# g_mem inside the memory chunks, row blocks turned between products, identity transposes ahead of the first product

## The chip, the cores and the metric

The kernel runs on one core of a Trainium2 chip. The metric is the device time of one execution in microseconds, median of three runs. The engines have short names in the profile: PE is TensorE (PEld its weight loads), DVE VectorE, ACT ScalarE, POOL GpSimd, SP SyncE, which issues most DMA transfers.

## The reference

One decoder layer in float32: a sequence of 512 rows of 1024 columns (`x`), and 256 memory rows (`mem`). The lines that the change touches:

```python
h = rms_norm(x, g_mix[l])
proj = h @ w_in[l]
q, k, v, qi, ki, wi, conv_in, qc, gate_pre = split_cols(proj, PROJ_SIZES)
qi = partial_rope(qi.reshape(b, s, N_IDX_HEADS, IDX_DIM), cos_i, sin_i)
ki = partial_rope(ki, cos_i, sin_i)
y_att = dsa_attention(q, k, v, qi, ki, wi) @ w_att_out[l]
mem_kv = (rms_norm(mem, g_mem[l]) @ w_mem_kv[l]).reshape(b, m, 2, N_CROSS_HEADS, HEAD_DIM)
y_mem = memory_attention(qc, mem_kv[:, :, 0], mem_kv[:, :, 1]) @ w_mem_out[l]
```

Behind them come a short convolution branch, three gates, the output product `w_o`, and a gated convolutional MLP (`w_up`, `w_down`). `rms_norm(x, g)` is `x * rsqrt(mean(x*x) + eps) * g`.

## The kernel before

Every matrix product is made of three TensorE matmuls (`mm3`, L145): both operands are split into a rounded half `hi` (ScalarE) and a remainder `lo` (VectorE), and hi x hi, hi x lo and lo x hi are added in one PSUM bank. A split (`split`, L155) is so one ScalarE and one VectorE instruction.

The work around the change is the start of the kernel, some 46 us:

- **Memory chunks.** `m_kv` holds, for each of the eight blocks of 128 rows of the contraction, 256 columns of `mem` transposed and 512 columns of `w_mem_kv`. It comes in five transfers (L255): the first two blocks singly, the others in pairs, called the first to fourth chunk here. For each block ScalarE and VectorE multiply the memory half by `gm`, a column of `g_mem` (L280, L281), and split the weights; then six products add to two banks `pkv`, one for each block of 128 memory rows. The norm's factor is put on later, in `memory_out` (L296).
- **Row blocks.** `x` comes in four blocks of 128 rows (`xin`). `norm_rows` (L165) normalises one: a sum of squares on ScalarE (L160), two small GpSimd steps (L161, L162), and one VectorE instruction (L170) that writes `xn`. `turn_rows` (L173) transposes it on TensorE, eight 128x128 transposes into two `at` banks, and splits the result into `h`. Block 0 is normalised and turned amid the memory chunks, block 1 behind them.
- **Row products.** The loop over b at L321 multiplies each block by `w_n`: 24 matmuls of 424 columns into a `mm` bank `pn`, which hold V, the index queries and keys, and the index weights `wiN`. At its end the loop normalises and turns block b + 2. ScalarE rounds V, copies the index rows to `rn` (L335), VectorE rotates them with the table `ropeN` in six small instructions (L338 to L343), and TensorE turns the result: the keys (L346, 32 columns) for each block, the queries (L349) for all but block 0. For blocks 0 and 1, `memory_out` is called as well, and its sum of squares over a memory block is the ScalarE instruction `rows<-rows` at L160.
- Behind it the first products with `w_in` begin (the operands come from `ahead`, L309); from there on TensorE runs the long products.

The order on each engine is set by a scheduler that places instructions by a simulated time and by priority (`tc.high_priority` raises the normalisation and the splits), except where `tc.keep_in_program_order` pins one: a pinned instruction isn't moved across the others of its engine that stand ahead of it in the program. An engine runs its instructions strictly in the order so made. DMA transfers use eight completion semaphores in turn, so that a transfer waits for the one eight places ahead of it.

Of the kernel before, what the change touches and what calls it, by code (L numbers as in the profile page):

```python
# [17 lines left out]
P = 128  # L18
S = 512
NB = S // P  # L20
# [72 lines left out]
@with_exitstack  # L93
def layer(ctx, tc, x, mem, g_mix, g_mem, g_ffn, g_final, w_in, w_n, m_kv, w_cm, w_att, w_o, w_up, w_down,
          params, rope, rope_n, out):
# [48 lines left out]

    def mm3(o, sh, sl, mh, ml, first, last):  # L145
        nc.tensor.matmul(o, sh, mh, start=first, stop=False)  # L146
        nc.tensor.matmul(o, sh, ml, start=False, stop=False)  # L147
        nc.tensor.matmul(o, sl, mh, start=False, stop=last)  # L148
# [23 lines left out]

    def turn_rows(xn, dst, b, tag="at"):  # L173

        for h in range(2):
            pt = bank(tag)
            for k in range(4):
                nc.tensor.transpose(pt[:, k * P:(k + 1) * P], xn[:, (4 * h + k) * P:(4 * h + k + 1) * P], ident)
            pv = pt.rearrange("p (k s) -> p k s", s=P)
            split(dst[0][:, 4 * h:4 * h + 4, b * P:(b + 1) * P], dst[1][:, 4 * h:4 * h + 4, b * P:(b + 1) * P], pv)  # L180
# [46 lines left out]
    ea = es.enter_context(pool("ea", side="right"))  # L227
    gm = ea.tile([P, KD], F32, name="gm")
    gx = ea.tile([P, D], F32, name="gx")
    ropeN = ea.tile([P, 2, NB, 4], F32, name="ropeN")  # L230
    nc.scalar.dma_start(gm, g_mem)
    nc.scalar.dma_start(ropeN, rope_n)

    warm = const.tile([P, 1], F32, name="warm")
    tc.keep_in_program_order(nc.scalar.activation(warm, mhalf, AF.Copy))


    def first(dma):
        tc.keep_in_program_order(dma)
# [10 lines left out]
    for c in range(KD // 2):  # L250

        n = 1 if c == 0 else 2
        raw = op.tile([P, 2, M + 2 * CW], F32, tag=kv_tags[c], name="mkv")
        for i in range(0, 2, n):
# [16 lines left out]
    xin.append(first_rows(x, 3, ea, "in3"))  # L271
    memn.append(first_rows(mem, 1, op, "omel"))


    pkv = [bank("o"), bank()]
    for c, (raw, hi, lo, n) in enumerate(mkv):
        for i in range(0, 2, n):
            for k in range(2 * c + i, 2 * c + i + n):
                src = raw[:, k % 2, :M]
                nc.scalar.activation(mh[:, k], src, AF.Copy, scale=gm[:, k:k + 1])  # L280
                nc.vector.scalar_tensor_tensor(ml[:, k], src, gm[:, k:k + 1], mh[:, k].bitcast(F32), op0=ALU.mult,  # L281
                                               op1=ALU.subtract)
            split(hi[:, i:i + n], lo[:, i:i + n], raw[:, i:i + n, M:])
            for k in range(2 * c + i, 2 * c + i + n):
                for b in range(MB):
                    bs = slice(b * P, (b + 1) * P)
                    mm3(pkv[b], mh[:, k, bs], ml[:, k, bs], hi[:, k % 2], lo[:, k % 2], k == 0, k == KD - 1)
        if c == 2:
            norm_T(xin[0], gx, h, 0, ea)
# [31 lines left out]
    for b in range(NB):  # L321
        bs = slice(b * P, (b + 1) * P)
        pn = bank()
        for i in range(4):
            for j in range(2):
                k = 2 * i + j
                mm3(pn[:, :NW], h[0][:, k, bs], h[1][:, k, bs], wn[i][1][:, j], wn[i][2][:, j], k == 0, k == KD - 1)
        if b + 2 < NB:
            with tc.high_priority(offset=800):
                norm_T(xin[b + 2], gx, h, b + 2, ea)  # L330
        split(V[:, b, :, 0:HD], V[:, b, :, HD:], pn[:, :KV].rearrange("p (g d) -> p g d", g=NG))
# [537 lines left out]
```

## Time and profile before

| | us |
|---|---|
| median of three runs | 756.78 (756.10 to 756.96) |
| profiled execution, its own time | 757.61 |
| span of the profiled execution | 755.8 |
| TensorE busy in the span | 740.9 |
| VectorE, ScalarE, GpSimd busy | 464.5, 340.2, 21.1 |

The profiled execution is 0.83 us above the median, and its span, from the first to the last instruction, is 1.8 us shorter than its own time. In the rows below, times are from the span's start; a matmul's duration includes the fill and drain of the array, so that consecutive matmuls overlap, and the distance of their starts is what one costs.

### The profile page before, as it was taken

The page shows a single profiled execution, that of the slowest core. Times are in us where ns is not written, and L with a number is a line of the kernel's source. Part 1 is how long each engine was busy: PE and PEld are TensorE (multiplying, and loading weights), DVE is VectorE, ACT ScalarE, POOL GpSimd, SP SyncE. Part 2 cuts the span into 40 slices and gives each one's busy share as a digit, 9 for nine tenths or more (in the row PEclk, how much of TensorE's full clock was granted, in tenths as well). Part 3 has the DMA queues.
Part 4 walks back from the last instruction along what each step waited for, and adds up shares of the span by engine and source line. Part 5 has one row for each costly group of instructions (what it writes and reads, how often), then busy time and mean ns, then how long its engine had stood idle before and what let it go on. Part 6 is the DMA issues. An engine that isn't in the chain of part 4 may idle for free.

```text
span 755.8 us, 9168 instructions
## 1 busy us (share of the span) xinstructions
PE 740.9 (98%) x3458; PEld 618.9 (82%) x3458; DVE 464.5 (61%) x795; ACT 340.2 (45%) x568; POOL 21.1 (3%) x49
## 2 busy tenths in 40 slices
PE   6999999999999999999999999999999999999996
PEld 4888888888888888888899888888888888888884
DVE  4845999999777763386466565656565654121225
ACT  5848565676455553244235434343434443121214
POOL 0200002000000000000010000000000000000001
PEclk9999999999999999999999999999999999999998
DMA  9625234522122224344403232232323232323202
GB/s 340 221 84 172 85 111 123 170 72 76 57 91 74 74 65 161 117 139 138 142 29 99 97 97 100 91 104 88 107 86 110 83 112 76 119 84 109 86 29 112
DMA packets 25709, 81.81 MB, mean 108 GB/s; under 512 B 3424, under 2 KB 4576, under 8 KB 25664
## 3 DMA queue, kind: packets, MB, share of 16 engines
q1 hardware_dynamic: 25232, 80.94, 32.7%
q8 instruction: 27, 0.44, 0.3%
q10 hardware_dynamic: 432, 0.28, 0.1%
q14 instruction: 18, 0.15, 0.1%
HBM read 75.77 MB, written 2.10 MB: 103 GB/s over the span
## 4 chain that ended last, share of the span: by engine, by line
PE 94%; ACT 2%; DMA 1%; DVE 1%; POOL 1%; issue 1%; POOLq 0%; SPq 0%
PE ps_mm L146 19%; PE ps_mm L148 19%; PE ps_mm L147 19%; PE ps_at L146 9%; PE ps_at L148 9%; PE ps_at L147 9%; PE ps_at L625 1%; PE ps_o L656 1%; DMA mkv<-m_kv 1%; PE ps_o L147 1%; PE ps_o L148 1%; PE ps_o L146 1%; PE ps_at L642 1%; PE ps_at L420 1%; PE ps_at L556 1%
## 5 line engine op out<-in xcount | busy, mean ns | idle before, releaser
L157 DVE TENSOR_TENSOR wlo<-raw,whi 128x1024 fp32r<-128x1024 f32 (+2 forms) x122 | 144.7, 1188 | 197.1 <-ACT whi L156 197.1
L156 ACT ACTIVATE whi<-raw 128x1024 fp32r<-128x1024 f32 (+2 forms) x122 | 125.8, 1032 | 177.1 <-PE ps_o L148 82.1
L146 PE MATMUL ps_mm<-hhi,whi 128*128 128x512 f32 x312 | 122.8, 394 | 0.0
L147 PE MATMUL ps_mm<-hlo,whi 128*128 128x512 f32 x312 | 122.2, 392 | 0.0
L148 PE MATMUL ps_mm<-hhi,wlo 128*128 128x512 f32 x312 | 122.2, 392 | 0.0
L147 PE MATMUL ps_at<-h2l,whi 128*128 128x512 f32 (+1 forms) x216 | 78.9, 366 | 0.0
L148 PE MATMUL ps_at<-h2h,wlo 128*128 128x512 f32 (+1 forms) x216 | 78.8, 365 | 0.0
L146 PE MATMUL ps_at<-h2h,whi 128*128 128x512 f32 (+1 forms) x216 | 78.7, 366 | 0.0
L148 PEld LDWEIGHTS ps_mm<-hhi,wlo 128*128 128x128 f32 x312 | 58.6, 188 | 11.7
L147 PEld LDWEIGHTS ps_mm<-hlo,whi 128*128 128x128 f32 x312 | 58.6, 188 | 11.6
L146 PEld LDWEIGHTS ps_mm<-hhi,whi 128*128 128x128 f32 x312 | 58.6, 188 | 11.5
L146 PE MATMUL ps_mm<-h2h,whi 128*128 128x512 f32 x160 | 62.2, 389 | 0.0
L147 PE MATMUL ps_mm<-h2l,whi 128*128 128x512 f32 x160 | 62.2, 389 | 0.0
L148 PE MATMUL ps_mm<-h2h,wlo 128*128 128x512 f32 x160 | 62.2, 389 | 0.0
L147 PEld LDWEIGHTS ps_at<-h2l,whi 128*128 128x128 f32 x216 | 40.7, 189 | 6.6
L148 PEld LDWEIGHTS ps_at<-h2h,wlo 128*128 128x128 f32 x216 | 40.7, 189 | 6.5
L146 PEld LDWEIGHTS ps_at<-h2h,whi 128*128 128x128 f32 x216 | 40.6, 189 | 6.5
L147 PEld LDWEIGHTS ps_mm<-h2l,whi 128*128 128x128 f32 x160 | 30.0, 188 | 6.3
L148 PEld LDWEIGHTS ps_mm<-h2h,wlo 128*128 128x128 f32 x160 | 30.0, 188 | 6.2
L146 PEld LDWEIGHTS ps_mm<-h2h,whi 128*128 128x128 f32 x160 | 30.0, 188 | 6.2
L789 ACT ACTIVATE t<-t 128x512 f32<-128x512 f32 x22 | 13.9, 633 | 44.9 <-DVE t L471 44.8
L156 ACT ACTIVATE acth<-t 128x512 fp32r<-128x512 f32 x14 | 8.8, 632 | 40.4 <-DVE t L790 40.4
(266 smaller groups left out, 1316.8 us busy)
## 6 DMA issues: line engine op xcount, KB each, us to landing
raw<-w_up SPq DMA_DIRECT2D x44, 512.0 KB, 3.4
raw<-w_in SPq DMA_DIRECT2D x39, 512.0 KB, 3.4
raw<-w_down SPq DMA_DIRECT2D x22, 512.0 KB, 3.4
raw<-w_o SPq DMA_DIRECT2D x8, 512.0 KB, 3.5
raw<-w_cm SPq DMA_DIRECT2D x8, 320.0 KB, 3.0
mkv<-m_kv SPq DMA_DIRECT2D x3, 768.0 KB, 8.8
rows<-x SPq DMA_DIRECT2D x4, 512.0 KB, 10.1
x<-x SPq DMA_DIRECT2D x4, 512.0 KB, 6.4
```

The lines of the kernel that those rows point to most:

```text
L146: nc.tensor.matmul(o, sh, mh, start=first, stop=False)
L147: nc.tensor.matmul(o, sh, ml, start=False, stop=False)
L148: nc.tensor.matmul(o, sl, mh, start=False, stop=last)
L156: nc.scalar.activation(hi, src, AF.Copy)
L157: nc.vector.tensor_sub(lo, src, hi.bitcast(F32))
L420: nc.tensor.matmul(pb[:, :W], Q4[:, hd, (b - 1) * P:b * P], K4[:, :W], start=True, stop=True)
L556: nc.tensor.matmul(pb[:, j * M:(j + 1) * M], QC[:, 2 * t + j, b * P:(b + 1) * P], KM[i][:, 2 * t + j, :], start=(i == 0), stop=(i == 1))
L625: nc.tensor.matmul(pb[:, :N], QS[:, hd, b * P:(b + 1) * P], KS[i][:, g, :N], start=(i == 0), stop=(i == 1))
L642: nc.tensor.transpose(pt[:, kb * P:(kb + 1) * P], lt[:, kb * P:(kb + 1) * P], ident)
L656: nc.tensor.matmul(po[:, q0:], V[:, kb, g, :], PT[i][:, c], start=(kb == 0 and i == 0), stop=(kb == NB - 1 and i == 1))
L789: nc.scalar.activation(tt[0], tt[0], AF.Silu)
```

## The change

Four edits, all in the start of the kernel:

1. `g_mem` is no longer a table of its own. Each row of `m_kv` gets one more column that holds it, so that a row is 769 instead of 768 numbers long; the instructions at L280 and L281 (L287, L288 after) read the factor from the chunk. The transfer of the table on ScalarE's queue is gone.
2. The transfer of the index rope table `ropeN` moves from the front of ScalarE's queue to the end of the start-up loads on SyncE's, behind the last memory block and ahead of the parameters `par`.
3. Fifteen TensorE transposes of the identity into an `at` bank that nothing reads stand ahead of the first product.
4. Blocks 2 and 3 are normalised in the loop rounds b = 1 and b = 2, ahead of that round's products, and turned in the middle of them, behind the first 12 (before: at the end of rounds 0 and 1). The first transpose of each half, and the first matmul behind the turn, are pinned to their place in the program.

```diff
--- before.py
+++ after.py
@@ -91,7 +91,7 @@
 
 
 @with_exitstack
-def layer(ctx, tc, x, mem, g_mix, g_mem, g_ffn, g_final, w_in, w_n, m_kv, w_cm, w_att, w_o, w_up, w_down,
+def layer(ctx, tc, x, mem, g_mix, g_ffn, g_final, w_in, w_n, m_kv, w_cm, w_att, w_o, w_up, w_down,
           params, rope, rope_n, out):
     nc = tc.nc
 
@@ -142,8 +142,10 @@
     def wrows(w, r, sp=wp):
         return wsplit(w[r * P:(r + 1) * P, :].rearrange("p (k c) -> p k c", c=P), sp)
 
-    def mm3(o, sh, sl, mh, ml, first, last):
-        nc.tensor.matmul(o, sh, mh, start=first, stop=False)
+    def mm3(o, sh, sl, mh, ml, first, last, pin=False):
+        mm = nc.tensor.matmul(o, sh, mh, start=first, stop=False)
+        if pin:
+            tc.keep_in_program_order(mm)
         nc.tensor.matmul(o, sh, ml, start=False, stop=False)
         nc.tensor.matmul(o, sl, mh, start=False, stop=last)
 
@@ -170,12 +172,14 @@
         nc.vector.scalar_tensor_tensor(xn, src, r, g, op0=ALU.mult, op1=ALU.mult)
         return xn
 
-    def turn_rows(xn, dst, b, tag="at"):
+    def turn_rows(xn, dst, b, tag="at", pin=False):
 
         for h in range(2):
             pt = bank(tag)
             for k in range(4):
-                nc.tensor.transpose(pt[:, k * P:(k + 1) * P], xn[:, (4 * h + k) * P:(4 * h + k + 1) * P], ident)
+                mm = nc.tensor.transpose(pt[:, k * P:(k + 1) * P], xn[:, (4 * h + k) * P:(4 * h + k + 1) * P], ident)
+                if pin and k == 0:
+                    tc.keep_in_program_order(mm)
             pv = pt.rearrange("p (k s) -> p k s", s=P)
             split(dst[0][:, 4 * h:4 * h + 4, b * P:(b + 1) * P], dst[1][:, 4 * h:4 * h + 4, b * P:(b + 1) * P], pv)
 
@@ -225,14 +229,16 @@
 
     es = ExitStack()
     ea = es.enter_context(pool("ea", side="right"))
-    gm = ea.tile([P, KD], F32, name="gm")
     gx = ea.tile([P, D], F32, name="gx")
     ropeN = ea.tile([P, 2, NB, 4], F32, name="ropeN")
-    nc.scalar.dma_start(gm, g_mem)
-    nc.scalar.dma_start(ropeN, rope_n)
 
     warm = const.tile([P, 1], F32, name="warm")
     tc.keep_in_program_order(nc.scalar.activation(warm, mhalf, AF.Copy))
+
+
+    idle = bank("at")
+    for i in range(15):
+        nc.tensor.transpose(idle[:, :P], ident, ident)
 
 
     def first(dma):
@@ -250,7 +256,7 @@
     for c in range(KD // 2):
 
         n = 1 if c == 0 else 2
-        raw = op.tile([P, 2, M + 2 * CW], F32, tag=kv_tags[c], name="mkv")
+        raw = op.tile([P, 2, M + 2 * CW + 1], F32, tag=kv_tags[c], name="mkv")
         for i in range(0, 2, n):
             first(nc.sync.dma_start(raw[:, i:i + n], m_kv[2 * c + i:2 * c + i + n].rearrange("k p c -> p k c")))
         hi = wp.tile([P, 2, 2 * CW], F32R, tag="whi", name="whi", bufs=3)
@@ -270,17 +276,18 @@
     memn = [first_rows(mem, 0, op, "omeh")]
     xin.append(first_rows(x, 3, ea, "in3"))
     memn.append(first_rows(mem, 1, op, "omel"))
+    first(nc.sync.dma_start(ropeN, rope_n))
 
 
     pkv = [bank("o"), bank()]
     for c, (raw, hi, lo, n) in enumerate(mkv):
         for i in range(0, 2, n):
             for k in range(2 * c + i, 2 * c + i + n):
-                src = raw[:, k % 2, :M]
-                nc.scalar.activation(mh[:, k], src, AF.Copy, scale=gm[:, k:k + 1])
-                nc.vector.scalar_tensor_tensor(ml[:, k], src, gm[:, k:k + 1], mh[:, k].bitcast(F32), op0=ALU.mult,
+                src, gm = raw[:, k % 2, :M], raw[:, k % 2, M + 2 * CW:]
+                nc.scalar.activation(mh[:, k], src, AF.Copy, scale=gm)
+                nc.vector.scalar_tensor_tensor(ml[:, k], src, gm, mh[:, k].bitcast(F32), op0=ALU.mult,
                                                op1=ALU.subtract)
-            split(hi[:, i:i + n], lo[:, i:i + n], raw[:, i:i + n, M:])
+            split(hi[:, i:i + n], lo[:, i:i + n], raw[:, i:i + n, M:M + 2 * CW])
             for k in range(2 * c + i, 2 * c + i + n):
                 for b in range(MB):
                     bs = slice(b * P, (b + 1) * P)
@@ -321,13 +328,18 @@
     for b in range(NB):
         bs = slice(b * P, (b + 1) * P)
         pn = bank()
+        nxt = xin[b + 1] if 0 < b < NB - 1 else None
+        if nxt is not None:
+            with tc.high_priority(offset=800):
+                nxt = norm_rows(nxt, gx, ea)
         for i in range(4):
+            if nxt is not None and i == 2:
+
+                turn_rows(nxt, h, b + 1, "at", pin=True)
             for j in range(2):
                 k = 2 * i + j
-                mm3(pn[:, :NW], h[0][:, k, bs], h[1][:, k, bs], wn[i][1][:, j], wn[i][2][:, j], k == 0, k == KD - 1)
-        if b + 2 < NB:
-            with tc.high_priority(offset=800):
-                norm_T(xin[b + 2], gx, h, b + 2, ea)
+                mm3(pn[:, :NW], h[0][:, k, bs], h[1][:, k, bs], wn[i][1][:, j], wn[i][2][:, j], k == 0, k == KD - 1,
+                    pin=nxt is not None and k == 4)
         split(V[:, b, :, 0:HD], V[:, b, :, HD:], pn[:, :KV].rearrange("p (g d) -> p g d", g=NG))
         nc.vector.tensor_scalar_mul(wiN[:, b, :], pn[:, NW - NIH:NW], (NIH * IDXD) ** -0.5)
         rn = ea.tile([P, NIH + 1, IDXD], F32, tag="rn", name="rn", bufs=2)
@@ -845,14 +857,14 @@
     add("x", w["x"])
     add("mem", w["mem"])
     add("g_mix", w["g_mix"].reshape(1, D))
-    add("g_mem", w["g_mem"].reshape(KD, P).T)
     for n in ("g_ffn", "g_final"):
         add(n, w[n].reshape(1, D))
     wide = range(0, D, P)
     add("w_in", col_blocks(w["w_in"], IN_STARTS))
     add("w_n", np.stack([col_blocks(w["w_in"][i:i + 2 * P], [C_V], NW)[0] for i in range(0, D, 2 * P)]))
 
-    add("m_kv", np.concatenate([w["mem"].reshape(M, KD, P).transpose(1, 2, 0), w["w_mem_kv"].reshape(KD, P, 2 * CW)], axis=2))
+    add("m_kv", np.concatenate([w["mem"].reshape(M, KD, P).transpose(1, 2, 0), w["w_mem_kv"].reshape(KD, P, 2 * CW),
+                                w["g_mem"].reshape(KD, P, 1)], axis=2))
     add("w_cm", np.concatenate([col_blocks(w["w_conv_out"], wide), col_blocks(w["w_mem_out"], wide)], axis=2))
     add("w_att", col_blocks(w["w_att_out"], range(0, D, 2 * P), 2 * P))
     add("w_o", w["w_o"])
```

TensorE in the loop over row blocks, around the turn of block 2, in the kernel before (`wnh`, `wnl` are the split of `w_n`, `rn` the rotated index rows, here of block 0, `xn` the normalised block):

```order
L147 MATMUL ps_mm<-wnl_155,hhi 128x424
L148 MATMUL ps_mm<-wnh_154,hlo 128x424
L178 MATMUL ps_at<-ident,xn 128x128 x8
L346 MATMUL ps_at<-ident,rn 32x128
L178 MATMUL ps_at<-ident,xn 128x128 x4
L146 MATMUL ps_mm<-wnh_142,hhi 128x424
L147 MATMUL ps_mm<-wnl_143,hhi 128x424
L178 MATMUL ps_at<-ident,xn 128x128 x4
```

The same place after the change:

```order
L149 MATMUL ps_mm<-wnl_160,hhi 128x424
L150 MATMUL ps_mm<-wnh_159,hlo 128x424
L358 MATMUL ps_at<-ident,rn 32x128
L180 MATMUL ps_at<-ident,xn 128x128 x8
L146 MATMUL ps_mm<-wnh_163,hhi 128x424
L149 MATMUL ps_mm<-wnl_164,hhi 128x424
L150 MATMUL ps_mm<-wnh_163,hlo 128x424
```

Before, all of block 1's products (the last with `wnh_154`) stand ahead of the turn of block 2 and of L346, and the turn of block 3 is broken by block 2's first products. After, only 12 of block 1's 24 products stand ahead, then L358 (L346 before), then the turn of block 2, then block 1's other 12 products.

VectorE at the same time, before:

```order
L365 TENSOR_SCALAR par<-par 128x24
L170 SCALAR_TENSOR_TENSOR xn<-rows,st,gx 128x1024
L338 TENSOR_TENSOR rt<-rn,ropeN 128x36
L339 TENSOR_TENSOR rt<-rn,ropeN 128x36
L341 TENSOR_TENSOR rn<-rn,ropeN 128x9x4
L340 TENSOR_TENSOR rn<-rn,ropeN 128x9x4
L343 TENSOR_TENSOR rn<-rn,rt 128x9x4
L342 TENSOR_TENSOR rn<-rn,rt 128x9x4
```

And after:

```order
L377 TENSOR_SCALAR par<-par 128x24
L350 TENSOR_TENSOR rt<-rn,ropeN 128x36
L351 TENSOR_TENSOR rt<-rn,ropeN 128x36
L353 TENSOR_TENSOR rn<-rn,ropeN 128x9x4
L352 TENSOR_TENSOR rn<-rn,ropeN 128x9x4
L172 SCALAR_TENSOR_TENSOR xn<-rows,st,gx 128x1024
L355 TENSOR_TENSOR rn<-rn,rt 128x9x4
L354 TENSOR_TENSOR rn<-rn,rt 128x9x4
```

The normalisation of row block 3 (`xn`) moves from ahead of block 0's rotation to between its fourth and its fifth step. On ScalarE the sums of squares of a memory block and of the row block beside it change places, twice: `rows<-rows` now stands ahead of `xn<-rows`. Behind the first group of `w_in` products all engines have the same order in both kernels.

## Rows read from the trace of the kernel before

**Rows 1.** The page: span, TensorE, its clock by slice, the second small DMA queue.

```profile
span 755.8 us, 9168 instructions
...
PE 740.9 (98%) x3458; PEld 618.9 (82%) x3458; DVE 464.5 (61%) x795; ACT 340.2 (45%) x568; POOL 21.1 (3%) x49
...
PEclk9999999999999999999999999999999999999998
...
q10 hardware_dynamic: 432, 0.28, 0.1%
```

**Rows 2.** Stretches: length; PE, PEld, DVE, ACT, POOL busy (instructions); PEclk, DMA share, GB/s.

```profile
4.80:10.90 6.10, 5.49 (x12) 3.80 (x12) 2.64 (x6) 2.88 (x5) 0.00 (x0) 1.00 1.02 374
...
18.00:20.00 2.00, 1.61 (x9) 1.08 (x8) 1.77 (x2) 2.00 (x5) 0.22 (x2) 1.00 1.03 419
...
45.50:748.50 703.00, 703.00 (x3279) 586.61 (x3277) 434.95 (x733) 310.75 (x511) 13.38 (x27) 1.00 0.31 100
748.50:751.00 2.50, 0.01 (x1) 0.00 (x0) 1.54 (x5) 1.26 (x4) 0.73 (x1) 1.00 0.53 210
751.00:752.00 1.00, 0.00 (x0) 0.00 (x0) 0.75 (x1) 0.72 (x1) 0.20 (x1) 0.71 0.02 8
```

**Rows 3.** Timeline, TensorE, start: start, duration, line, operation, [idle before <- releaser].

```profile
4.83 0.79 PE L146 MATMUL ps_o<-whi,mT 128*128 128x512 f32 x1 [4.83 <-ACT mT L280]
...
9.69 0.63 PE L148 MATMUL ps_mm<-whi,mT 128*128 128x512 f32 x1
10.94 0.50 PE L146 MATMUL ps_o<-whi,mT 128*128 128x512 f32 x1 [0.62 <-ACT whi L156]
...
12.20 0.50 PE L147 MATMUL ps_o<-wlo,mT 128*128 128x512 f32 x1 [0.53 <-DVE wlo L157]
```

**Rows 4.** Timeline, GpSimd's identity and ScalarE's second chunk.

```profile
1.14 0.29 POOL masks.py:199 TENSOR_SCALAR_AFFINE_SELECT ident<-ident 128x128 f32<-128x128 f32 x1
...
9.04 0.91 ACT L280 ACTIVATE mT<-mkv,gm 128x256 fp32r<-128x256 f32 x2 [3.20 <-DMA mkv<-m_kv]
```

**Rows 5.** Timeline, TensorE, the row blocks' products and turns.

```profile
27.77 0.55 PE L148 MATMUL ps_mm<-wnh,hlo 128*128 128x424 f32 x2
...
29.91 0.35 PE L146 MATMUL ps_mm<-wnh,hhi 128*128 128x424 f32 x1
...
32.23 1.04 PE L178 MATMUL ps_at<-ident,xn 128*128 128x128 f32 x8
33.11 0.27 PE L346 MATMUL ps_at<-ident,rn 128*32 128x128 f32 x1
...
34.93 0.46 PE L146 MATMUL ps_mm<-wnh,hhi 128*128 128x424 f32 x1 [1.12 <-ACT hhi L156]
...
45.56 0.39 PE L147 MATMUL ps_mm<-hlo,whi 128*128 128x512 f32 x1
45.79 0.40 PE L148 MATMUL ps_mm<-hhi,wlo 128*128 128x512 f32 x1
```

**Rows 6.** Timeline, ScalarE, GpSimd and VectorE around block 0's index rows.

```profile
30.33 0.20 ACT L160 ACTIVATION_READ_ACCUMULATOR rows<-rows 128x1 f32 x1
30.43 0.41 ACT L335 ACTIVATE rn<-ps_mm 128x288 f32<-128x288 f32 x1
...
29.58 0.19 POOL L161 TENSOR_SCALAR st<-st 128x1 f32<-128x1 f32 x1 [2.17 <-ACT xn L160]
29.86 0.55 POOL L162 TENSOR_TENSOR st<-st,mhalf 128x1 f32<-128x1 f32 x1
30.62 1.16 POOL L161 TENSOR_SCALAR st<-st 128x1 f32<-128x1 f32 x1 [0.21 <-ACT rows L160]
...
30.44 1.28 DVE L170 SCALAR_TENSOR_TENSOR xn<-rows,st,gx 128x1024 f32<-128x1024 f32 x1 [1.21 <-POOL st L162]
31.64 0.19 DVE L338 TENSOR_TENSOR rt<-rn,ropeN 128x36 f32<-128x36 f32 x1
...
32.24 0.19 DVE L342 TENSOR_TENSOR rn<-rn,rt 128x36 f32<-128x36 f32 x1
```

## The prediction

> **What bounds the kernel now.** The page comes first: TensorE is busy for 740.9 of the span's 755.8 us [rows 1]. The table of stretches then says where it isn't: from 45.5 to 748.5 us it is busy for all 703.0 us, so whatever TensorE loses or gains before 45.5 us reaches the end one for one, and nothing later takes it up [rows 2]. The change works only ahead of that point, so I read the first 46 us row by row. There TensorE loses time in three places. It has nothing until 4.83 us. It waits at 10.94 and 12.20 us for the second memory chunk [rows 3], and that wait goes back to a transfer: ScalarE sat 3.20 us until the chunk landed at 9.04 us [rows 4]. Last, at 34.93 us, it waits 1.12 us for the ScalarE half of row block 2's split, right after turning that block [rows 5]. The profiled execution lasted 757.61 us with its span of 755.8; the median of the three runs is 756.78. I make the sum as a difference on the span and put it on the median.
>
> **The identity transposes.** The first 12 products (those of the first two chunk rows) start at 4.83 and the last of them at 9.69 us, 0.44 us apart; later ones are 0.23 us apart (45.56 to 45.79) [rows 3, 5]. The page's clock row and the stretch 4.80 to 10.90 both print full clock there [rows 1, 2], but 512 columns in 0.43 us is the lower level of 1.2 GHz, and 0.23 us is the 2.4 GHz one. So the low clock costs 12 x 0.20 = 2.4 us of TensorE time. None of that is on the path: if the 12 products took 2.7 us instead of 5.1, TensorE would be done near 8 us and still could not go on before 10.94 us, because the chunk lands at 9.04 us and its first multiply-and-round and its split take until 10.9 us [rows 3, 4]. Gain taken: 0. The price of the 15 transposes themselves: the identity is written at 1.43 us [rows 4]; eight transposes at the high clock start 0.11 us apart (32.23 to 33.11) [rows 5], so 15 at half the clock take about 3.3 us and end near 4.9 us, 0 to 0.4 us after the operands; the slack of 0.62 us ahead of 10.94 us hides that [rows 3]. The transposes are TensorE's own; no other engine waits for them.
>
> The Trainium skill's page "TensorE: Matmul & The Clock Gate", in Part 4 on transposes, says that transpose mode does not count as TensorE activity for the clock in the way matmuls do. No row of before shows the clock's answer to transposes alone. By that rule the first 12 products stay slow and the sum of this part is the same 0, since the wait for the chunk takes up either case; what it alters is the chance of the clock rival below, where transposes follow a wait.
>
> **g_mem in the chunks, the rope table last.** Two ScalarE-queue transfers of 128 small packets each go away at the front, 16 KB of them come back at the end of the start-up queue, ahead of the parameters. All small packets of that queue, with the last output among them, are 432 packets in 0.1% of sixteen engines' span [rows 1], so 0.75 us at most for all, of which the two tables can be some 0.2 us; that comes off the landing of every chunk. Against it the chunk's rows grow from 3072 to 3076 bytes. Rows of w_n, 3392 bytes, move at 419 GB/s between 18 and 20 us, no slower than anything else [rows 2]; I take 0, with 0.4 us as the dear end (5% of the four chunks of 768 KB at that rate). The table now follows the load of the last memory block on SyncE's queue; ScalarE takes that block's sum of squares ahead of the copy at 30.43 us, and the table, 16 KB, is first read after that copy (31.64 us before) [rows 6], so it isn't late. Sum taken: -0.1 us, from -0.4 to +0.4.
>
> The page "DMA: Bandwidth & Descriptors", section "How a descriptor splits into AXI transactions", of the Trainium skill says that a descriptor which does not start on a 256-byte boundary spends extra beats. An estimate from it is about 4 beats on 96, near 0.4 us by the fourth chunk, which would be the dear end; the 419 GB/s of the 3392-byte rows speak against it.
>
> **Row blocks turned amid the products.** This part decides. In the order of before, TensorE runs all 24 products of block 1, turns block 2, and only then turns the rotated index row of block 0 (L346). In the new order the first of the pinned transposes keeps its program place, and so everything that stands ahead of it in the program must run ahead of it: the transpose of block 0's rotated keys, L358, now comes after only 12 of block 1's products, and the turn of block 2 and all else queues behind it. TensorE gets there at 29.91 us (the thirteenth product's start in before) [rows 5]. Are the rotated keys ready? Follow the chain. Block 0's last product starts at 27.77 us [rows 5]. After rounding its V, ScalarE's order holds two sums of squares (now memory block 1 first, row block 3 second) ahead of the copy L347, so that the copy runs at 30.43 us as before and the second sum is read out at 30.53 us [rows 6]. VectorE's order now holds four of the six rotation steps, then the normalisation of row block 3, then the last two steps, where before all six stood together. The normalisation waits for GpSimd, whose two steps for the row sum before took 0.83 us (29.58 to 29.86 + 0.55) [rows 6]: 30.6 + 0.85 = 31.45 us. The normalisation takes 1.20 us of VectorE (30.44 to 31.64), the last two steps 0.3 us (32.24 us is the start of the last, and each starts 0.11 us after the other) [rows 6]: 31.5 + 1.2 + 0.3 = 33.0 us. With the hand-over L358 starts at 33.05 us. **The wait is 33.05 - 29.91 = 3.1 us.** Its bounds: 1.75 us if the normalisation cost nothing (copy 30.43 + 0.41, six steps of 0.12, a hand-over), 4.1 us if GpSimd's first step takes the 1.16 us that it took beside a VectorE normalisation [rows 6].
>
> What goes away: from 29.91 to 45.56 us are 15.65 us [rows 5]. The work in it is 60 products of 424 columns, 11.6 us at 0.194 (the starts at 27.77 and 29.91 are 11 products apart) [rows 5], 16 turns at 0.11 = 1.8, four rotated-row turns 0.35, one product of 512 columns 0.23: 14.0 us. So before loses 1.65 us there, 1.12 in the wait at 34.93 and the rest in restarts after waits. After: that goes, since 12 products (2.3 us) now stand between the turn and its first reader, twice the 1.12 us that it waited. In comes 3.1 us, and some 0.3 us for restarts. For block 1's rotated rows, ahead of the turn of block 3, the same chain without sums or normalisation in it is about 2.2 us against 2.3 us of products: 0 to 0.2 us, 0.1 taken. **Sum: +3.1 + 0.3 + 0.1 - 1.65 - 0.1 = +1.75 us, which gives 756.78 + 1.75 = 758.5 us.** Behind L358 nothing but TensorE's own queue waits; ScalarE and VectorE have the first w_in split to do meanwhile.
>
> **Rivals.** (1) The wait is there and the clock falls in it. After the last product of the kernel (about 748.5 us) the clock was lower from within 751 to 752 us on, after less than 3 us without a matmul [rows 2]; a wait of 3.1 us followed by 1 us of transposes is of that size. Against it: waits of 0.62 and 1.12 us left the clock up. Its price: a 424-column product takes 0.35 instead of 0.19 us, and if the low clock lasts as long as at the start, 5.5 us or 15 products, that is 2.4 us; half of it is possible. 760.0 to 761.0 us, 760.4 as its own time. The Trainium skill's page "TensorE: Matmul & The Clock Gate", section "HAM oscillation — how this bites in real kernels", says that where matmul bursts are parted by long enough waits, each next burst starts slow; the end of this trace agrees, with the fall to 1.2 GHz after under 3 us of no matmul.
>
> (2) The change does what it is named for and the rope rows are there in time: the 1.65 us of lost time goes, 0.1 us on the transfers, and nothing new comes. 755.0 us. For it: the 1.12 us wait is real and 12 products would cover it. Against it: the copy L347 cannot run before ScalarE has done the two sums, so that L358 is late by 1.75 us even at the lower bound; it decides only if L358's operand is ready by 31.5 us.
>
> (3) The wait comes out at its lower end, near 2 us, because VectorE finishes the rotation before GpSimd is done, or the start gains up to 0.4 us: 756.5 to 757.8 us, no change that can be told.
>
> (4) The faster first 12 products leave TensorE idle for some 2 to 3 us ahead of 10.94 us, and the clock falls there, so that the products from 12.20 us on start slow: up to 2.4 us on top of the forecast, 1.8 taken. 760.3 us.
>
> **How the numbers follow.** Forecast, the wait with the clock up: 45%, 758.5 us, its own range 757.8 to 759.4. Rival 1: 32%. Rival 4: 5%. Rival 3: 12%. Rival 2: 6%. The range from 757.2 to 761.2 us leaves out rival 2, half of rival 3 and the upper tail of the clock. About 0.2%, 1.5 us, is what a measurement of this kernel can tell from no change; the forecast lies just beyond it, so a third of its 45% counts as no change. Slower 0.67, the same 0.26, faster 0.07.
>
> **What would show it.** In the trace of the changed kernel: the first 12 products 0.43 or 0.23 us apart, and the next one at 10.5 to 11.3 us either way; L358 starting 2 to 4 us after the product ahead of it, released by VectorE's L354 or L355, with VectorE's normalisation L172 between L352 and L355; no wait of over 0.3 us ahead of block 2's first product; the spacing of the 424-column products after L358, 0.19 us (forecast) or 0.35 us (rival 1). The forecast falls if L358 waits less than 1.5 us, or if TensorE isn't busy throughout after 48 us.

## The result, and the profile after

The changed kernel takes 761.66 us (median; 759.87 to 761.73) where the kernel before takes 756.87 beside it: a ratio of 1.0059, with a 95% interval from 1.0042 to 1.0076. That is slower by 3.2 to 5.8 us. The direction was forecast, the size (+1.75 us) wasn't, and the time lies above the range. The profiled execution took 761.6 us with a span of 759.8. Two executions of the experiments below, of 829.8 us (e7) and 4286.69 us (e11), lie far outside the rest and are in no ratio.

The page, as in [rows 1]: the span, and TensorE with its share.

```profile
span 759.8 us, 9193 instructions
...
PE 744.6 (98%) x3473; PEld 622.2 (82%) x3473; DVE 464.9 (61%) x795; ACT 340.6 (45%) x568; POOL 20.1 (3%) x49
```

TensorE is busy 3.7 us longer than before, but 3.46 us of that are the 15 new transposes at the start, in time that was idle before. So the sum of the busy time doesn't price the loss, which must be looked for in the distance of the starts as well as in idle time.

The start, TensorE in order of time (start, duration, line, operation, idle before and what ended it), answering to [rows 3]:

```profile
1.48 3.46 PE L241 MATMUL ps_at<-ident 128*128 128x128 f32 x15 [1.48 <-POOL ident masks.py:199]
4.96 0.80 PE L146 MATMUL ps_o<-whi,mT 128*128 128x512 f32 x1
...
5.98 0.60 PE L149 MATMUL ps_o<-wlo,mT 128*128 128x512 f32 x1
6.41 0.40 PE L150 MATMUL ps_o<-whi,mT 128*128 128x512 f32 x1
...
8.27 0.39 PE L150 MATMUL ps_mm<-whi,mT 128*128 128x512 f32 x1
10.65 0.50 PE L146 MATMUL ps_o<-whi,mT 128*128 128x512 f32 x1 [1.99 <-ACT whi L158]
```

The first products start 0.43 us apart (5.98 to 6.41), the later ones 0.23 (6.41 to 8.27 is eight of them). The clock rose 1.5 us after the first product; before, it was still low 4.9 us after it [rows 3]. Nothing comes of it: TensorE then idles 1.99 us where it idled 0.62.

The wait, on TensorE, answering to [rows 5]:

```profile
29.50 0.36 PE L150 MATMUL ps_mm<-wnh,hlo 128*128 128x424 f32 x1
33.36 0.27 PE L358 MATMUL ps_at<-ident,rn 128*32 128x128 f32 x1 [3.51 <-DVE rn L354]
33.47 1.66 PE L180 MATMUL ps_at<-ident,xn 128*128 128x128 f32 x8
34.78 0.70 PE L146 MATMUL ps_mm<-wnh,hhi 128*128 128x424 f32 x1
35.28 0.56 PE L149 MATMUL ps_mm<-wnl,hhi 128*128 128x424 f32 x1
35.63 0.56 PE L150 MATMUL ps_mm<-wnh,hlo 128*128 128x424 f32 x1
...
37.05 0.40 PE L146 MATMUL ps_mm<-wnh,hhi 128*128 128x424 f32 x1
37.29 0.35 PE L149 MATMUL ps_mm<-wnl,hhi 128*128 128x424 f32 x1
```

L358, the transpose of block 0's rotated keys, stands behind the twelfth product of block 1 and waits 3.51 us, as the order of the program said it would. Behind it the products are 0.35 us apart (0.50 the first time) until 37.05 us, and 0.18 to 0.24 from there on. Those are the two levels, 1.2 and 2.4 GHz. The table of stretches prints the granted clock of the same place (stretch; length, TensorE busy, instructions; granted clock, DMA share, GB/s):

```profile
33.40:37.10 3.70, 3.70 (x16) 0.54 0.34 105
```

The chain that L358 waits for, ScalarE, then GpSimd, then VectorE, answering to [rows 6]:

```profile
28.56 1.06 ACT L162 ACTIVATE rows<-rows 128x1024 f32<-128x1024 f32 x1 [0.34 <-DVE xn L172]
...
30.66 0.39 ACT L347 ACTIVATE rn<-ps_mm 128x288 f32<-128x288 f32 x1
...
30.84 0.19 POOL L163 TENSOR_SCALAR st<-st 128x1 f32<-128x1 f32 x1 [0.22 <-ACT xn L162]
31.11 0.57 POOL L164 TENSOR_TENSOR st<-st,mhalf 128x1 f32<-128x1 f32 x1
...
31.71 1.28 DVE L172 SCALAR_TENSOR_TENSOR xn<-rows,st,gx 128x1024 f32<-128x1024 f32 x1
32.92 0.19 DVE L355 TENSOR_TENSOR rn<-rn,rt 128x36 f32<-128x36 f32 x1
33.02 0.19 DVE L354 TENSOR_TENSOR rn<-rn,rt 128x36 f32<-128x36 f32 x1
```

Every member is where the prediction put it: two sums of squares, then the copy; the sum's two GpSimd steps, 0.84 us; the normalisation between the fourth and the fifth step of the rotation; the last two steps.

From here to the end two rows mark the way, the product that in before starts at 45.79 us [rows 5], and the last product of the kernel. The second one in before:

```profile
748.12 0.39 PE L148 MATMUL ps_o<-whi,actl 128*128 128x512 f32 x1
```

Both after the change:

```profile
49.17 0.39 PE L150 MATMUL ps_mm<-hhi,wlo 128*128 128x512 f32 x1
...
752.19 0.39 PE L150 MATMUL ps_o<-whi,actl 128*128 128x512 f32 x1
```

So 3.38 us are lost by 49.17 us, and 4.07 by the last product. The way between the two marks took 702.33 us before and takes 703.02 now. The prediction had said that nothing there would change.

### The profile page after: what moved, and what is told of

Read it like the earlier page. It is cut to its first block, busy times and chain, and to the rows that moved or that the text cites. A ratio compares the mean times of both kernels' runs of the same rounds, so it can differ in the third digit from the quotient of the medians.

```text
span 759.8 us, 9193 instructions
## 1 busy us (share of the span) xinstructions
PE 744.6 (98%) x3473; PEld 622.2 (82%) x3473; DVE 464.9 (61%) x795; ACT 340.6 (45%) x568; POOL 20.1 (3%) x49
## 4 chain that ended last, share of the span: by engine, by line
PE 94%; ACT 2%; DVE 1%; DMA 1%; issue 1%; POOL 1%; POOLq 0%; SPq 0%; ACTq 0%
PE ps_mm L149 19%; PE ps_mm L150 19%; PE ps_mm L146 19%; PE ps_at L146 9%; PE ps_at L149 9%; PE ps_at L150 9%; PE ps_at L637 1%; PE ps_o L668 1%; PE ps_o L149 1%; DMA mkv<-m_kv 1%; PE ps_o L150 1%; PE ps_o L146 1%; PE ps_at L654 1%; PE ps_at L180 1%; PE ps_at L432 1%
```

## The experiments

Each was run beside the kernel before on the same chip. Ratios are to that kernel, with 95% intervals. Labels are the runs' names. "Marks" are the two products above.

**Is it the transpose in front of the pinned turn? (e1_rope_later)** The transposes of a block's rotated rows are emitted behind the next block's products.

```diff
+        if rope_due is not None:
+            turn_rope(*rope_due)
...
-        pt = bank("at")
-        nc.tensor.transpose(pt[:IDXD, 2 * P:3 * P], rows_[:, 2 * P:], ident)
...
+        rope_due = (b, rows_)
```

> The changed kernel, but the transposes of a block's rotated rows stand in the program behind the products of the next block, so that block 0's rotated keys no longer stand ahead of the pinned turn of block 2. Theory A (the keys' transpose, dragged ahead of the pinned turn, causes the wait of 3.51 us, and the clock falls in that wait in most executions): no wait at the turn of block 2, the clock stays at full speed behind it, the old wait of 1.12 us is gone too, and with the 0.2 us that the memory chunks' landing gives at the start the time is 754.8 to 755.6 us, below the kernel before (756.9). Theory B (the loss comes from the start, that is from the identity transposes, the idle behind them, or the longer chunk rows): still about 760 to 761.5 us. Theory C (without that wait the turn of block 2 waits for its own normalisation instead): 756.5 to 758, with a wait of 1 to 3 us ahead of the turn, released by VectorE's normalisation.

Measured: 758.07 against 757.07, ratio 1.0012 (1.0000 to 1.0023). The wait at the turn of block 2 is gone, and with it most of the loss, so theory A has the cause right and the sum wrong. Two things are left. The rotated keys are now dragged ahead of the next pinned turn, that of block 3, and wait there for 0.85 us. And in the profiled execution the clock fell at the start of the kernel:

```profile
10.72 0.50 PE L146 MATMUL ps_o<-whi,mT 128*128 128x512 f32 x1 [2.24 <-ACT whi L158]
...
13.09 0.63 PE L146 MATMUL ps_o<-whi,mT 128*128 128x512 f32 x1
13.52 0.63 PE L149 MATMUL ps_o<-wlo,mT 128*128 128x512 f32 x1
...
16.67 0.39 PE L150 MATMUL ps_o<-whi,mT 128*128 128x512 f32 x1
...
37.86 0.28 PE L330 MATMUL ps_at<-ident,rn 128*32 128x128 f32 x1 [0.85 <-DVE rn L370]
```

This is TensorE in order of time. After the idle of 2.24 us and the short one behind it, products are 0.43 us apart from 13.09 us on, and 0.23 again from 16.67 on. It isn't hidden: the last product of the chunks starts at 22.19 us here, and at 21.06 us in the changed kernel's profile. Six of the twelve executions, 758.52 us and above, have the lower mean clock (0.993 to 0.995).

**The start by itself (e2_no_row_part).** The loop of before, with the other three edits kept.

```diff
-        nxt = xin[b + 1] if 0 < b < NB - 1 else None
-        if nxt is not None:
-            with tc.high_priority(offset=800):
-                nxt = norm_rows(nxt, gx, ea)
...
-                turn_rows(nxt, h, b + 1, "at", pin=True)
...
+        if b + 2 < NB:
+            with tc.high_priority(offset=800):
+                norm_T(xin[b + 2], gx, h, b + 2, ea)
```

> The changed kernel with the row-block loop of before: only the identity transposes, g_mem in the chunks and the rope table at the end are left. Theory A (all of the loss is in the row-block part): 756.4 to 757.0 us, the same as before within 0.1%; block 0's last row product starts about 0.2 us earlier than in before (27.55 to 27.6 against 27.77 us), and the wait of about 1.1 us behind the turn of block 2 is back. Theory B (the start loses): 758.5 us or more. If the early rise of the clock were on the path, 755 us or less.

Measured: 758.07 against 757.07, ratio 1.0017 (1.0009 to 1.0026): the start loses 1.0 us by the medians and 1.3 by the ratio, so neither theory holds. The executions form two groups, seven at 757.55 to 758.10 us and five at 759.28 to 759.44 with a lower mean clock. Even the lower group is 0.8 us above before. Yet its profile reaches the first mark 0.39 us earlier than before (45.40 us), and loses 0.71 us between the marks (703.04 us). The first number says little, since e10 and e13 below, with the instructions of before, reach that mark 0.33 and 0.61 us earlier than before's one profile too. The loss is one of the long stages, where no instruction was changed.

**The row blocks by themselves (e3_row_part_only).** The kernel before with the fourth edit alone.

> The kernel before with the row-block part of the change alone. Theory A: like the whole change and 0.2 us later, with a wait of 3.4 to 3.7 us ahead of block 0's rotated keys and the clock at half speed for some 3.4 us behind it in most executions: 761 to 762 us, and 759.5 to 760.2 us in an execution whose clock holds. Theory B: 756.5 to 757.5 us. If the identity transposes at the start made the clock more ready to fall in the later wait, all executions would hold it here: 759.5 to 760.2 us.

Measured: 761.40 against 757.07, ratio 1.0055 (1.0043 to 1.0066). The wait is 3.52 us:

```profile
32.73 0.27 PE L355 MATMUL ps_at<-ident,rn 128*32 128x128 f32 x1 [3.52 <-DVE rn L351]
```

The clock falls behind it in the profile, and the mean clock of all six executions is low (0.993 to 0.996; 0.996 to 0.999 in nearly all of before), so the identity transposes are no part of that fall. Between the marks it takes 702.33 us, exactly as before: this edit costs nothing late.

**The wait filled (e4_fill, e12_fill_only).** Work that nothing reads is put into the wait, in the changed kernel and in the kernel with the row-block part alone.

```diff
+            if b == 1 and i == 2:
+                fill = bank("at")
+                for n in range(28):
+                    mm = nc.tensor.transpose(fill[:, :P], ident, ident)
+                    tc.keep_in_program_order(mm)
+                turn_rope(*rope_due, pin=True)
```

> The changed kernel with 28 more identity transposes (3.1 us of TensorE work that nothing reads) between block 1's twelfth product and the transpose of block 0's rotated keys, that is in the wait. If the wait is 3.5 us and the clock's fall comes from TensorE's idleness in it, and transposes keep the clock up: every execution is like the one of the changed kernel whose clock held, 759.7 to 760.2 us, with the products behind the turn 0.19 us apart. If transposes do not keep the clock up: 761.5 to 762 us, the products behind the turn 0.35 us apart. If the operand were ready earlier than the trace says: over 762 us, since the transposes would then be on the path themselves.

Measured: 760.75 against 757.07, ratio 1.0047 (1.0034 to 1.0060), in two groups, 759.8 to 760.2 and 761.3 to 761.6 us, three executions each. The lower one is where the first theory put it. The upper one may come from the fall at the start that e1 shows; no trace here shows it. So the fill was repeated on the start of before:

> The kernel before with the row-block part and 28 identity transposes in the wait for block 0's rotated keys; the start and the tiles' places are those of before. It prices the wait without the clock: the row-block part alone took 761.4 us where before took 757.07, with the clock falling in the wait. If the wait is worth 3.5 us less the 1.65 us that it replaces, with 0.5 us of restarts: 2.1 to 2.6 us above before, in one group, and no fall of the clock. If the clock falls all the same: 4 us above.

Measured: 759.37 against 757.15, ratio 1.0026 (1.0016 to 1.0036), seven of eight executions at 758.35 to 759.6. TensorE, in order of time:

```profile
29.49 3.22 PE L350 MATMUL ps_at<-ident 128*128 128x128 f32 x28
33.17 0.27 PE L327 MATMUL ps_at<-ident,rn 128*32 128x128 f32 x1 [0.46 <-DVE rn L371]
33.28 1.03 PE L180 MATMUL ps_at<-ident,xn 128*128 128x128 f32 x8
34.07 0.44 PE L146 MATMUL ps_mm<-wnh,hhi 128*128 128x424 f32 x1
34.34 0.35 PE L149 MATMUL ps_mm<-wnl,hhi 128*128 128x424 f32 x1
34.54 0.36 PE L150 MATMUL ps_mm<-wnh,hlo 128*128 128x424 f32 x1
...
47.41 0.39 PE L150 MATMUL ps_mm<-hhi,wlo 128*128 128x512 f32 x1
```

The keys are no earlier, but the products behind them stand 0.20 us apart at once. So the clock falls when TensorE has nothing to do in the wait, and stays up when it has transposes, and the wait without the clock costs 2.0 us by the ratio. In the traces the way from the keys' transpose to the first mark, with the same work in it, takes 14.24 us here (33.17 to 47.41) and 15.81 us in the changed kernel (33.36 to 49.17): the fall costs 1.6 us. By the ratios e3 lies 2.2 us above e12 (4.2 less 2.0, on two chips); the 0.6 us by which the two prices differ aren't explained. What made the eighth execution late (761.13 us, mean clock 0.996) no trace shows.

**The place of the tiles (e6_pad, e10_place_only, e13_place64).** A chunk tile in SBUF shares its place with a tile of the attention's or the convolution's output (`oath`, `oatl`, `ocvh` and `ocvl` are used in its stead later). Those are 6144 bytes a partition; 769 instead of 768 columns make it 6152, which is rounded to 6176. So `oath`, the first, keeps its place, `oatl` moves by 32 bytes, and the tiles behind it by twice, three times, four times that. The split weights lie in another pool (`wp`), ahead of this one, and don't move. e6 is e2 with tiles 784 columns wide, a step of 128 bytes:

```diff
-        raw = op.tile([P, 2, M + 2 * CW + 1], F32, tag=kv_tags[c], name="mkv")
+        raw = op.tile([P, 2, M + 2 * CW + 16], F32, tag=kv_tags[c], name="mkv")
```

> The kernel without the row-block part (g_mem in the chunks, rope table last, identity transposes), but each chunk tile in SBUF is 784 instead of 769 columns wide, of which 769 are filled: the tiles that share its pool lie 128 bytes (times 0 to 4) from their place in the kernel before, instead of 32. With 769 columns the products of w_cm's end and of w_att stood 0.230 to 0.233 us apart, in before 0.227, and 0.5 us was lost from 321 to 344 us. Theory P (the tiles' place is the cause): 0.227 us again there, the loss gone, the undisturbed executions at 757.0 to 757.3 us (757.55 to 758.1 without the padding). Theory Q (a matter of when the stage starts, or of the semaphores' turn): 0.230 us or more again and 757.5 to 758.1 us. Either way some executions 1.5 us later, if the identity transposes make the clock fall at the start.

Measured: 758.32 against 756.32, ratio 1.0024 (1.0012 to 1.0036), but with three of seven executions at 756.4 to 757.06 and the others 1.5 us and more later, so the time says little. The profile says more: 702.56 us between the marks, where e2 had 703.04. e10 asks the question alone: the kernel before, no transfer and no instruction changed, the chunk tile one unused column wider.

```diff
-        raw = op.tile([P, 2, M + 2 * CW], F32, tag=kv_tags[c], name="mkv")
+        raw = op.tile([P, 2, M + 2 * CW + 1], F32, tag=kv_tags[c], name="mkv")
```

> The kernel before, with the chunk tiles in SBUF 769 columns wide of which 768 are filled and read: no transfer and no instruction is changed, only the tiles that share the pool lie 32 bytes (times 0 to 4) further. If their place costs time by itself: the products of the memory chunks and those of w_cm's end and w_att 0.230 to 0.233 us apart as in the changed kernel, and the time 0.6 to 0.9 us above before (757.0 to 757.3 against 756.4 on the chip of the last comparison). If the loss comes from the longer rows in DRAM or from the changed transfers: like before, within 0.2 us, 0.227 us apart.

Measured: 758.04 against 757.15, ratio 1.0015 (1.0006 to 1.0024), and 703.05 us between the marks:

```profile
45.46 0.40 PE L148 MATMUL ps_mm<-hhi,wlo 128*128 128x512 f32 x1
...
748.51 0.39 PE L148 MATMUL ps_o<-whi,actl 128*128 128x512 f32 x1
```

That is 0.72 us more than before, the whole late loss. It goes with the place in every profile: the five with the 32-byte step (changed kernel, e1, e2, e4, e10) take 703.02 to 703.05 us, the four with the places of before (before, e3, e8, e12) 702.33 or 702.34. Only e11 can't be compared so, since it puts other work ahead of the first mark. TensorE's groups from 325.5 to 342 us, the products of `w_att`, in which `oath` and `oatl` stream past the weights, show it in before, e10 and e6, in this order (line, operation, shapes, count | busy us, mean ns | idle us):

```profile
L147 PE MATMUL ps_mm<-oatl,whi 128*128 128x512 f32 x21 | 8.2, 389 | 0.0
L148 PE MATMUL ps_mm<-oath,wlo 128*128 128x512 f32 x21 | 8.2, 389 | 0.0
L146 PE MATMUL ps_mm<-oath,whi 128*128 128x512 f32 x20 | 7.8, 389 | 0.0
```

```profile
L148 PE MATMUL ps_mm<-oath,wlo 128*128 128x512 f32 x21 | 8.2, 393 | 0.0
L147 PE MATMUL ps_mm<-oatl,whi 128*128 128x512 f32 x20 | 7.9, 395 | 0.0
L146 PE MATMUL ps_mm<-oath,whi 128*128 128x512 f32 x20 | 7.9, 394 | 0.0
```

```profile
L149 PE MATMUL ps_mm<-oatl,whi 128*128 128x512 f32 x21 | 8.3, 395 | 0.0
L146 PE MATMUL ps_mm<-oath,whi 128*128 128x512 f32 x20 | 7.8, 389 | 0.0
L150 PE MATMUL ps_mm<-oath,wlo 128*128 128x512 f32 x20 | 7.8, 388 | 0.0
```

Each product is 4 to 6 ns dearer with the 32-byte step, and with 128 bytes only one in three is. The engine shows no idle time in any of them. The products with the other tiles of this pool, the outputs of convolution and memory, are dearer as well; one group of them from 240 to 345 us, in before and in e10:

```profile
L147 PE MATMUL ps_mm<-ocvl,whi 128*128 128x512 f32 x15 | 5.9, 391 | 0.0
```

```profile
L147 PE MATMUL ps_mm<-ocvl,whi 128*128 128x512 f32 x15 | 5.9, 396 | 0.0
```

Over all 192 products that stream a tile of this pool, the distances of the starts add up to 0.81 us more than before in e10 and 0.24 in e6, so the late loss lies in them. The place of the streamed tile alone doesn't explain it, since `oath` hasn't moved in e10 and its products are dearer too. The last of these runs tried 64 bytes:

> The kernel before, with the chunk tiles 776 columns wide of which 768 are filled and read, so that the tiles of the shared pool lie 64 bytes (times 0 to 4) from their place in before. With a step of 32 bytes the time rose by 0.9 us (ratio 1.0015) and the products of w_att stood 0.231 us apart; with a step of 128 bytes they stood 0.2285 us apart. If it matters on which side of a 64-byte line a tile begins: 0.227 to 0.2285 us apart and at most 0.4 us above before. If any move of the tiles costs it: 0.231 us and 0.9 us.

Measured: 757.90 against 757.19, ratio 1.0009 (0.9999 to 1.0018); 703.14 us between the marks. The guess that a 64-byte line decides is refuted: 64 bytes cost 0.8 us between the marks, like 32; the times alone wouldn't tell it from none. Why the place matters isn't settled.

**The other two edits of the start (e7_pad_noidle, e8_idle_only).** e7 is e6 without the identity transposes; e8 is the kernel before with them alone.

> The same without the identity transposes: g_mem in the padded chunk tiles and the rope table last alone. If the identity transposes cause the second, later group of executions (759.3 to 759.4 us; the clock fell at 12.95 us in a profiled execution of that kind), that group is gone here, and the time is 756.6 to 757.2 us in one group; if the chunks cause it, it stays. The first products stand 0.43 us apart until 9 us and the wait ahead of the second chunk is 0.5 us or less.

Measured: 757.21 against 756.32, ratio 1.0011 (1.0002 to 1.0019), in one group (756.38 to 757.66). The later group is far more frequent with the identity transposes: 5 of 12 executions in e2 and 4 of 7 in e6, and none of the ten here. It isn't theirs alone, since 4 of the 94 executions of before that ran beside the experiments and 2 of the 11 of e10 are some 2 us late too, at a mean clock of 0.994 or 0.995. That 0.9 us remain where the place now costs 0.2 between the marks isn't explained; its profile came to the first mark only 0.13 us earlier than before's.

> The kernel before with the 15 identity transposes alone. If they are what makes the clock fall behind the early idle: two groups of executions, one like before (756.5 to 757.2 us), the other 1.5 us later (758.2 to 758.8), with the second group 3 to 7 times in 12. If not: one group at 756.5 to 757.2 us. In the profile the clock rises at 6 to 7.5 us instead of 10 to 11, and TensorE then waits 1.4 to 2.3 us for the second chunk.

Measured: 756.31 against 756.32, ratio 1.0007 (0.9998 to 1.0016). Nine of eleven executions stand between 755.67 and 757.40 us, two at 757.95 and 758.44 with the lower clock: no gain, and now and then the clock's price. The second group is rarer than expected (2 of 11). Its profile shows what the transposes do to the clock:

```profile
1.49 3.23 PE L240 MATMUL ps_at<-ident 128*128 128x128 f32 x15 [1.49 <-POOL ident masks.py:199]
4.96 0.50 PE L146 MATMUL ps_o<-whi,mT 128*128 128x512 f32 x1 [0.24 <-ACT mT L285]
5.29 0.39 PE L146 MATMUL ps_mm<-whi,mT 128*128 128x512 f32 x1
5.52 0.39 PE L147 MATMUL ps_o<-wlo,mT 128*128 128x512 f32 x1
```

The very first products are already 0.23 us apart (5.29 to 5.52), with nothing but transposes ahead of them.

**Two candidates (e9_best, e11_rows_fixed).** e9 joins e7 and e1.

> The candidate: g_mem in padded chunk tiles, rope table last, no identity transposes, blocks 2 and 3 turned amid the products, and the rotated rows of a block turned behind the products of the next. No wait at the turn of block 2, at most 0.9 us ahead of block 0's rotated keys, no fall of the clock: 755.0 to 756.0 us, in one group, against 756.9 of the kernel before. If the turning amid the products is worth nothing without the wait: 756.5 to 757.0 us.

Measured: 756.44 against 756.32, ratio 1.0001 (0.9992 to 1.0009). It has the 0.87 us wait at the turn of block 3, and whatever e7 loses. e11 drops the first three edits and turns a block's rotated rows two rounds later, so that they stand behind both pinned turns:

```diff
+        if b > 1:
+            turn_rope(*rope_due.pop(0))
...
-        rn = ea.tile([P, NIH + 1, IDXD], F32, tag="rn", name="rn", bufs=2)
+        rn = ea.tile([P, NIH + 1, IDXD], F32, tag="rn", name="rn", bufs=3)
```

> The kernel before with the row-block part alone, and a block's rotated rows turned two rounds later, behind the pinned turns. Nothing of the start is changed, no tile of the shared pool moves. If the wait and what follows from it were all that the row-block part cost, and its gain is the 1.65 us of lost time that the prediction counted: no wait of over 0.3 us between 28 and 46 us, no fall of the clock, and 1.4 to 1.7 us below before. If turning amid the products is worth only what the other candidate showed against its counterpart without it (0.7 us): 0.6 to 0.9 us below.

Measured: 755.49 against 757.15, ratio 0.9976 (0.9967 to 0.9985): faster than before by 1.7 us by the medians and 1.8 by the ratio. TensorE's stretch from 28 to 46 us, and the two turns in it:

```profile
28.00:46.00 18.00, 18.00 (x103) 1.00 0.23 80
```

```profile
29.74 1.03 PE L180 MATMUL ps_at<-ident,xn 128*128 128x128 f32 x8
...
35.24 1.03 PE L180 MATMUL ps_at<-ident,xn 128*128 128x128 f32 x8
```

TensorE is busy throughout. The turning amid the products is worth what it was meant to be; the change had put an operand that wasn't ready in front of it.

## Why the prediction was right or wrong

**That all is decided ahead of 45.5 us [rows 2]: wrong, by 0.7 us.** TensorE was busy throughout there, before and after, and I took that for a stage that can't change. What the start loses does reach the end one for one: e3 takes 702.33 us between the marks, like before. But the move of the tiles, for which the sum held nothing, lengthened the distance of the starts there, by some 5 ns a product in `w_att`.

**The identity transposes, gain 0: right.** The second chunk ended the wait at 10.65 us as said, and e8 takes the same time as before. Rival 4, the clock falling in the longer early idle, was given 5%: it didn't happen in the profiled execution, but did in e1's, and the upper groups of e2 (5 of 12) and e8 (2 of 11) are of its size, 1.5 us in e2 where I had 1.8.

**g_mem in the chunks and the rope table last, -0.1 us: wrong.** I priced the transfers' bytes, from -0.4 to +0.4, and not what a wider tile does to its neighbours' addresses. The place alone costs 0.9 us (e10). Transfers are no part of that, since e10 left them as they were; what they cost or save by themselves isn't shown, since e7's 0.9 us stay unexplained. The Trainium skill's page "SBUF — State Buffer", in "Operand start alignment", says that an operand may start at any multiple of its element size, and that this is about legality, not speed; here speed does depend on where tiles lie, by 0.7 us between the marks.

**The wait, 3.1 us: right in its cause, somewhat small.** TensorE would have gone on at 29.69 us (0.19 after 29.50) and went on at 33.36, 3.67 us later. Of the 0.53 us by which that is more, 0.22 are the earlier start of the row products in this execution (27.55 us, 27.77 in before), which the wait swallowed. It can't be put down to the change: in e3, e10, e12 and e13, with the instructions of before at the start, they stand at 26.93 to 27.43 us. The other 0.31 are the chain: the second sum of squares and the copy behind it ran 0.23 us late (the copy at 30.66 instead of 30.43 us), since ScalarE's first sum began late (0.34 us behind VectorE), and the rest is the hand-over. GpSimd's two steps (0.84 us against 0.85) and the normalisation's 1.21 us (31.71 to 32.92) are as forecast.

**What goes away, 1.65 us: right.** e11 gains 1.7 to 1.8 us. e12 prices the wait without the clock at +2.0 us, within the forecast's own range (+1.0 to +2.6).

**The clock: the step that failed.** I made the wait with the clock up the forecast (45%) and its fall a rival (32%), so that the sum held nothing for the clock. It fell in three of four executions of the changed kernel, and by their mean clock in all six of e3. From the profile the fall costs 1.5 us: the turn of block 2 took 1.31 us instead of 0.79 (33.47 to 34.78; 29.74 to 30.53 in e11), and six products at 0.38 us, 2.27 us, where they take 1.25 at 0.19 and a start. The way from the keys' transpose to the first mark gives 1.6. By the times it is more: the remaining execution, 759.87, is 1.8 below the others, and e3 less e12 gives 2.2. Rival 1's 2.4 us was a little dear, and its time of 760.4 was still too low, because the wait was 0.3 us longer at its end and the tiles' 0.7 us were in no sum. The rows had pointed to it: the clock was down 3 to 4 us after the last product of the kernel had started [rows 2], and I let waits of 0.62 and 1.12 us speak against it, a third of the one in question.

Added up for the profiled pair: -0.22 (earlier start) + 3.67 (wait) - 1.65 (old losses) + 1.5 (clock) = 3.3 us by 49.17 us, where 3.38 were read; with 0.7 for the tiles that is 4.0 by the last product, where 4.07 were read. The medians lie 4.8 us apart (4.5 by the ratio): the profiled execution of before is 0.7 us above its median and that of the changed kernel isn't, and where before lost it no trace shows. The wait ahead of block 1's rotated rows, 0.1 us in the sum, didn't come.

## What to carry to other kernels

An instruction pinned to its place drags everything ahead of it in the program with it: look, for each such instruction, whether all that stands before it is ready by then, and emit what isn't behind it. When a wait of some 3 us is put on TensorE's path, count the slow products behind it into the forecast, not into a rival. And a tile that grows by a few bytes moves its neighbours: keep the size of a shared place, or measure the move alone.

## What had not been expected of the hardware

- Where the tiles of one SBUF pool lie changes what the products that stream them past the weights take: 4 to 6 ns each in `w_att` with steps of 32 bytes, without idle time; with steps of 128 bytes one product in three. It was found by the place alone (e10: +0.72 us between the marks, and e13, with 64 bytes, +0.81). The weights didn't move, nor did `oath`, whose products are dearer too. The cause is open.
- The clock rises on identity transposes: in e8 it was up by the second product, where in before the first twelve were slow [rows 3]; in the changed kernel three were slow. The Trainium skill's page "TensorE: Matmul & The Clock Gate", in Part 4 on PE-mode transposes, says that these don't count as activity in the same way. Here they did, and in e12 28 of them, 3.22 us long, kept it up through the wait.
- The same fall isn't taken in every execution: 759.87 us (mean clock 0.998) and 761.7 us (0.994 to 0.996) are the same program.
